# Two transformer blocks on one core: operand tiles at multiples of 512 bytes, and the second block's constants made in its own phase

## The chip, the cores and the metric

The kernel runs on one core of one Trainium2 chip. The metric is the device time of one execution in microseconds. Before the change the median of three runs is 2538.58 us (2537.44 to 2539.23).

## The reference

Two transformer blocks work one after the other on x, 256 tokens by 2,048 features, in fp32. Each block makes six modulation vectors from a condition c by a product of silu(c) with a 2,048 x 12,288 matrix ("ada"), normalizes and modulates x, mixes the tokens, adds the result through a gate, and then does the same with a feed-forward layer of width 8,192.

```python
# first block
mod = silu(c) @ w_ada + b_ada
h = rms_norm(x, norm1_w) * (1 + scale1) + shift1
u_pool, q, k, v, g_a, g_b = split(h @ w_in)
y_a = multiscale_pool(u_pool, w_pool, pool_scale) @ w_a_up
y_b = stick_breaking_attention(rms_norm(q), rms_norm(k), v) @ w_b_up
x = x + gate1 * ((sigmoid(g_a) * y_a + sigmoid(g_b) * y_b) @ w_o)
h2 = rms_norm(x, norm2_w) * (1 + scale2) + shift2
x = x + gate2 * (square(relu(h2 @ w_ff1)) @ w_ff2)
# second block: the same frame; the mixer is
attn = rms_norm(dilated_attention(rope(rms_norm(aq)), rope(rms_norm(ak)), av))
ho = hgrn2(gq, gf, gi, lb)          # gated recurrence; lb is the floor of its forget gate
mix = concat(attn, rms_norm(ho) * silu(gg)) @ w_out
```

## The kernel before, in words

*The products.* All large products stream the weights. A weight block of 128 partitions x 4 x 512 columns (1 MB) is loaded from HBM into a `raw` tile (4 buffers, `pump`, line 163, queue of SP). Half a block at a time is split into two parts whose sum it is: `hi`, the rounded part, by a copy on ScalarE (line 199), and `lo`, the rest, by a subtraction on VectorE (line 207); there are four buffers of each. The activations are split in the same way, transposed to [feature, token], and kept in tiles `act` (modulated norm, and the operand of the output projections), `f` (hidden activations of the feed-forward layers), `pT` (pooling), `oT` (stick-breaking attention) and `m0` (a part of the second block's mixer). `unit` (line 292) issues, for each of the two token tiles, three matmuls of 128 x 128 weights against 512 columns: line 301 takes the activation's high part as weights and `hi` as the moving operand, line 302 the high part and `lo`, line 303 the low part and `hi`. A half block is two contraction tiles, so 12 matmuls.

*The order.* `run` (line 243) emits the program by half blocks. Before each one it runs the functions that `at` registered for it, steps the generators in `side` (spawned work such as attention heads), and prepares `hi` and `lo` up to three half blocks ahead (`LOOK`). Around a norm four half blocks are taken together, one token tile after the other. The modulation vectors are products on VectorE (`ada_product`, line 175) that are spread over the weight blocks.

*The constants of the second block.* `block2_consts` (line 879) is a generator that is spawned at half block 40 of the first feed-forward layer (line 1419). It loads masks (`lvl`, `cnt`), positions, inverse frequencies and rotary weights by five DMAs on SP's queue, converts the masks on VectorE, builds the rotary tables (`rope`, two sines on ScalarE) and the floor of the forget gate (`lb`). Results lie in the pool `fix2`, opened at the start of the first feed-forward layer (line 408) and kept to the end; scratch is a tile `consts` of the pool `t2p`.

*The stick-breaking heads* (`sb_head`, line 846) work in a tile of three rows of 384 columns: e, lb and lm. The sums over later keys are a product of lm with the triangle `tri` and with the matrix `ones`, two of the three 128-column parts of `cst`, whose first is the identity `ident` of all transposes.

*Where tiles lie.* A pool's tiles lie one behind the other in the order of their first request, pools in the order in which they are opened; each tile's size is rounded up to 32 bytes. The fixed pool begins at byte 16,512 of each partition, with `cb` (8,192 bytes), `x` (16,384), `pkt` (1,184), `cst` (1,536). The starts of the operand tiles in the program of the kernel before:

| tile | role on lines 301 to 303 | first byte | modulo 512 |
|---|---|---|---|
| hi (4 buffers x 2 halves) | moving | 79,168 and on by 2,048 | 320 |
| lo (4 buffers x 2 halves) | moving | 95,552 and on by 2,048 | 320 |
| act (4 tiles) | weights | 128,320 and on by 8,192 | 320 |
| oT (2 tiles) | weights | 202,048 and 210,240 | 320 |
| pT (in the place of x) | weights | 24,704 | 128 |
| f (4 tiles) | weights | 172,000 and on by 8,192 | 480 |
| m0 (2 tiles) | weights | 172,000 and 180,192 | 480 |

Within a tile all slices that are taken as weights or as moving operand start at multiples of 512 bytes from its first byte. Memory ends at byte 229,376; the last tile of the first block's mixer ends at 229,184, the gate of the feed-forward layers at 229,344.

Of the kernel before, what the change touches and what calls it, by code (L numbers as in the profile page):

```python
# [18 lines left out]
P = 128  # L19
# [14 lines left out]
# packed parameter columns: name -> (first column, columns)  # L34
# [29 lines left out]
class Net:  # L64
    def __init__(self, ctx, tc, A):
# [10 lines left out]
        self.scope = ctx.enter_context(ExitStack())  # L76
        self.side = []
# [48 lines left out]
    def add_block(self, src, units):  # L126
        """units: four (segment, k) pairs, in the order of the block's 512-column tiles."""
# [13 lines left out]
    def add_pair(self, srcs, a, b):  # L141
        """Two segments side by side, two contraction tiles of each in turn."""
# [38 lines left out]
    def prep_hi(self):  # L181
        """The first part of the next half block; what stands before it in the queue is used first."""
# [20 lines left out]
    def prep_lo(self):  # L203
        """The rest of that half block."""
# [16 lines left out]
    def interleave(self, plan):  # L221
        """Spread the vector products over the weight blocks: (first block, blocks per product, items)."""
# [89 lines left out]
    def act_tiles(self):  # L312
        """Lazily allocated [feature, token] operand of 16 contraction tiles, split in two parts."""
# [12 lines left out]
    def rstd(self, ss, n, d, out=None):  # L326
        """(ss/d + eps)^-1/2 of a [128, n] tile of sums of squares, with a Newton step."""
# [13 lines left out]
    def split_to(self, src, dst):  # L341
        """Transpose four 128-column tiles of src [token, feature] into dst [feature, 4, 2, token]."""
# [7 lines left out]
    def gate_rows(self, col, dst):  # L350
        """dst[:, n] = gate n on every partition, from gate columns [128, 16]."""
# [9 lines left out]
    def mod_cols(self, mod, b, j0, name):  # L361
        """mod + b_ada columns j0..j0+15."""
# [4 lines left out]
    def load_c2(self):  # L367
        """c_2 on every partition, in the place of c."""
# [15 lines left out]
    def residual(self, g, a, tt, gate, norm=None):  # L384
        """x[:, group g] += gate * acc for one token tile; sums of squares for the norm that follows."""
# [13 lines left out]
    def ffn(self, w1p, w1, w2, norm, mod, b, ada_base, next_norm=None, out=None):  # L399
# [83 lines left out]
    def setup(self):  # L483
        nc, fix, A = self.nc, self.fix, self.A
        # silu(c) on every partition: the row times a column of ones
# [16 lines left out]
        self.cst = fix.tile([P, 3, P], F32, tag="cst", name="cst")  # L502
# [4 lines left out]
        self.ident, self.tri, self.ones = (self.cst[:, i, :] for i in range(3))  # L507
# [15 lines left out]
    def block1(self):  # L523
# [9 lines left out]
        # ---- normalized x, transposed; its modulation arrives tile by tile  # L533
# [34 lines left out]
        # ---- twelve column groups, a chunk of the contraction tiles at a time  # L568
# [5 lines left out]
        def part(key):  # L574
            """Where the sums of a group are kept between its contraction chunks: [token, 2, 512]."""
# [49 lines left out]
        # where the vector products of the later chunks stand: first block, blocks per product  # L625
# [72 lines left out]
        # ---- output projection  # L698
# [62 lines left out]
    def pool_loads(self, i):  # L761
        """Half of the pooling weights; the window matrices with the first."""
# [19 lines left out]
    def pool_group(self, g, u, pT):  # L782
        """Windowed means minus the token, then the group's map, times the scale, in two parts."""
# [47 lines left out]
    def heads(self, hs, every, make):  # L831
        """Run the heads' generators, a new one every so many steps, at most two at once."""
# [13 lines left out]
    def sb_head(self, h, qkT, v, o32):  # L846
# [8 lines left out]
        w = mp.tile([P, 3, 384], F32, tag="band" if h % 2 else "wp", name="sbw")  # L855
        yield
        e, lb, lm = (w[:, i, :] for i in range(3))
# [20 lines left out]

    def block2_consts(self):
        """Masks, rotary tables, the decay floor: everything of the second block that is small."""  # L880
        nc, fix, A = self.nc, self.fix2, self.A
        self.lvl = fix.tile([P, 7, 64], U8, tag="lvl", name="lvl")
# [10 lines left out]
        pos = fix.tile([P, 2], I32, tag="pos", name="pos")  # L893
        nc.sync.dma_start(out=pos, in_=A["positions"])
        tmp = self.t2(name="consts")
        w = tmp[:, 0:192].rearrange("p (a t f) -> p a t f", a=6, t=2)
        inv = tmp[:, 192:208]
        nw = tmp[:, 208:272].rearrange("p (a f) -> p a f", a=2)
# [650 lines left out]
```

## Time and profile before

| | us |
|---|---|
| median of three runs | 2538.58 |
| lowest and highest | 2537.44, 2539.23 |
| span of the profiled execution | 2536.3 |
| TensorE busy | 2505.9 |
| VectorE busy | 1808.3 |
| ScalarE busy | 1268.3 |

The span is the time from the first to the last instruction of one profiled execution, which is some 2 us less than the time of a run. The busy time of TensorE counts a matmul from its start to the modelled end of its last result, so that neighbours overlap: the recorded duration of a matmul (some 390 ns) is longer than the distance from its start to the start of the next (some 230 ns), and the throughput is read from the starts. Weight loads have rows of their own (PEld). In the rows below, a stretch shows its start and end, its us, the busy us and instructions of TensorE, its weight loads, VectorE, ScalarE and GpSimd, then the granted share of TensorE's clock, the DMA engines' busy share and GB/s; where it is of one tile alone, VectorE and ScalarE only.

### The profile page before, as it was taken

The page shows a single profiled execution, that of the slowest core. Times are in us where ns is not written, and L with a number is a line of the kernel's source. Part 1 is how long each engine was busy: PE and PEld are TensorE (multiplying, and loading weights), DVE is VectorE, ACT ScalarE, POOL GpSimd, SP SyncE. Part 2 cuts the span into 40 slices and gives each one's busy share as a digit, 9 for nine tenths or more (in the row PEclk, how much of TensorE's full clock was granted, in tenths as well). Part 3 has the DMA queues.
Part 4 walks back from the last instruction along what each step waited for, and adds up shares of the span by engine and source line. Part 5 has one row for each costly group of instructions (what it writes and reads, how often), then busy time and mean ns, then how long its engine had stood idle before and what let it go on. Part 6 is the DMA issues. An engine that isn't in the chain of part 4 may idle for free.

```text
span 2536.3 us, 29315 instructions
## 1 busy us (share of the span) xinstructions
PE 2505.9 (99%) x11392; PEld 2052.5 (81%) x11392; DVE 1808.3 (71%) x2121; ACT 1268.3 (50%) x1740; POOL 4.0 (0%) x8
## 2 busy tenths in 40 slices
PE   7999999999999999999999999999999999999999
PEld 5778888887888888888887888888788888888887
DVE  7897888888866677787777878766666554446554
ACT  5536545445545534534446656565554453443442
POOL 0000000000000000000000000000000000000000
PEclk9999999999999999999999999999999999999999
DMA  9988678977877777787766564665576755555553
GB/s 358 374 321 317 241 298 316 396 283 286 303 306 291 297 298 299 288 324 300 297 266 239 226 231 184 234 231 215 200 265 253 271 189 183 182 184 194 186 191 124
DMA packets 92876, 662.08 MB, mean 261 GB/s; under 512 B 10689, under 2 KB 11329, under 8 KB 12737
## 3 DMA queue, kind: packets, MB, share of 16 engines
q1 hardware_dynamic: 92738, 660.22, 68.8%
q8 instruction: 89, 1.46, 0.2%
q14 instruction: 49, 0.40, 0.0%
HBM read 655.99 MB, written 4.19 MB: 260 GB/s over the span
## 4 chain that ended last, share of the span: by engine, by line
PE 90%; DVE 6%; ACT 2%; issue 1%; DMA 1%; SPq 0%; ACTq 0%; DVEq 0%
PE acc L303 28%; PE acc L302 28%; PE acc L301 28%; DVE ada L175 2%; DVE lo L207 2%; PE ms L346 1%; ACT hi L199 1%; PE ms L1169 1%; PE ms L850 1%; PE ms L1283 0%; DMA raw<-in_win 0%; ACT hm L1387 0%; PE ms L1401 0%; PE ms L357 0%; PE ms L757 0%
## 5 line engine op out<-in xcount | busy, mean ns | idle before, releaser
L207 DVE TENSOR_TENSOR lo<-raw,hi 128x1024 fp32r<-128x1024 f32 x848 | 1027.9, 1223 | 615.6 <-ACT hi L199 612.7
L199 ACT CAST hi<-raw 128x1024 fp32r<-128x1024 f32 x848 | 883.0, 1049 | 879.8 <-PE acc L303 831.4
L301 PE MATMUL acc<-hi,act 128*128 128x512 f32 x2208 | 875.6, 397 | 8.0 <-ACT hi L199 6.9
L302 PE MATMUL acc<-lo,act 128*128 128x512 f32 x2208 | 863.8, 391 | 9.2 <-DVE lo L207 9.2
L303 PE MATMUL acc<-hi,act 128*128 128x512 f32 x2208 | 862.8, 391 | 0.0
L302 PEld LDWEIGHTS acc<-lo,act 128*128 128x128 f32 x2208 | 416.0, 188 | 98.5 <-DVE lo L207 16.5
L301 PEld LDWEIGHTS acc<-hi,act 128*128 128x128 f32 x2208 | 415.7, 188 | 93.7 <-ACT hi L199 8.8
L303 PEld LDWEIGHTS acc<-hi,act 128*128 128x128 f32 x2208 | 415.6, 188 | 88.2 <-DVE act L1392 0.7
L175 DVE CUSTOM_DVE_ANT_0 ada<-ada,cb 128x2048 f32<-128x2048 f32 x192 | 438.2, 2284 | 0.0
L303 PE MATMUL acc<-hi,f 128*128 128x512 f32 x1024 | 408.3, 399 | 0.0
L302 PE MATMUL acc<-lo,f 128*128 128x512 f32 x1024 | 403.6, 394 | 0.0
L301 PE MATMUL acc<-hi,f 128*128 128x512 f32 x1024 | 402.3, 393 | 0.0
L302 PEld LDWEIGHTS acc<-lo,f 128*128 128x128 f32 x1024 | 192.3, 188 | 49.4
L301 PEld LDWEIGHTS acc<-hi,f 128*128 128x128 f32 x1024 | 192.2, 188 | 45.6
L303 PEld LDWEIGHTS acc<-hi,f 128*128 128x128 f32 x1024 | 192.2, 188 | 44.3
L380 ACT ACTIVATE act<-xT,sAB 128x256 fp32r<-128x256 f32 x16 | 9.6, 601 | 86.9 <-DVE sAB L560 86.9
L418 ACT ACTIVATE relu<-acc 128x512 f32<-128x512 f32 x64 | 37.7, 590 | 29.0 <-PE acc L303 29.0
L348 DVE TENSOR_TENSOR f<-ms,f 128x512 fp32r<-128x512 f32 x64 | 41.1, 683 | 3.7 <-ACT f L347 3.7
L391 DVE TENSOR_TENSOR res<-acc,gate 128x512 f32<-128x512 f32 x32 | 22.0, 688 | 29.9 <-PE acc L303 29.9
L394 ACT ACTIVATE res<-x 128x512 f32<-128x512 f32 x24 | 15.2, 632 | 53.1 <-DVE x L392 53.1
L347 ACT CAST f<-ms 128x512 fp32r<-128x512 f32 x64 | 34.4, 589 | 14.5 <-PE ms L346 14.5
L419 ACT ACTIVATE relu<-relu 128x512 f32<-128x512 f32 x64 | 40.5, 633 | 2.0
(242 smaller groups left out, 1292.8 us busy)
## 6 DMA issues: line engine op xcount, KB each, us to landing
raw<-in_ff SPq DMA_DIRECT2D x240, 1024.0 KB, 5.8
ada<-in_ada SPq DMA_DIRECT2D x192, 1024.0 KB, 5.9
raw<-in_win SPq DMA_DIRECT2D x120, 1024.0 KB, 6.7
raw<-in_ff1p SPq DMA_DIRECT2D x16, 1024.0 KB, 5.5
raw<-in_wa SPq DMA_DIRECT2D x8, 1024.0 KB, 6.9
raw<-in_wb SPq DMA_DIRECT2D x8, 1024.0 KB, 9.5
raw<-in_wop SPq DMA_DIRECT2D x8, 1024.0 KB, 6.9
raw<-in_wo SPq DMA_DIRECT2D x8, 1024.0 KB, 8.6
```

The costliest lines, as they stand in the source:

```text
L175: self.nc.vector.tensor_tensor_reduce(out=t, in0=t, in1=cb(), scale=1.0, scalar=0.0, op0=ALU.mult, op1=ALU.add, accum_out=mod[:, j:j + 1])
L199: self.nc.scalar.copy(hi, src)
L207: self.nc.vector.tensor_tensor(out=lo, in0=src, in1=hi.bitcast(F32), op=ALU.subtract)
L301: self.nc.tensor.matmul(a, xh, hi, start=first, stop=False)
L302: self.nc.tensor.matmul(a, xh, lo, start=False, stop=False)
L303: self.nc.tensor.matmul(a, xl, hi, start=False, stop=last)
L346: nc.tensor.transpose(ps[:, i, :], src[:, i * P:(i + 1) * P], self.ident)
L347: nc.scalar.copy(dst[:, :, 0, :], ps)
L348: nc.vector.tensor_tensor(out=dst[:, :, 1, :], in0=ps, in1=dst[:, :, 0, :].bitcast(F32), op=ALU.subtract)
L418: nc.scalar.activation(r, acc[tt], AF.Relu)
L419: nc.scalar.activation(r, r, AF.Square)
L850: mm = lambda *a, **kw: nc.tensor.matmul(*a, skip_group_check=True, **kw)
```

## The change

Unnamed padding tiles of 96 and 72 columns are put into the fixed pool; `cst` loses its third part, in whose place `ones` becomes a column of ones that is read with step 0. The heads' tile has two rows instead of three: lm is written into e, and the sum goes into lb. The pool `fix2` is opened with the second block's phase (and lives as long as that), with a padding tile of 88 columns at its head; `block2_consts` is spawned at the second block's first half block, with its scratch in a tile under the tag of the later `A1` (1,536 columns). In it the five DMAs come first, then the floor `lb`, then the masks, then the rotary tables. The comments and docstrings that the diff also removes are left out here.

```diff
@@ Net.__init__
         self.scope = ctx.enter_context(ExitStack())
+        self.fix.tile([P, 96], F32, tag="pad0", name="pad")
@@ ffn
         def pools():
-            self.scope.close()
-            if ada_base == 0:
-                self.fix2 = self.ctx.enter_context(self.tc.tile_pool(name="fix2", bufs=1))
             self.phase(fp=4, ffp=1)
@@ setup
         self.pkt = fix.tile([P, NPK], F32, tag="pk", name="pkt")
-        self.cst = fix.tile([P, 3, P], F32, tag="cst", name="cst")
+        fix.tile([P, 72], F32, tag="pad1", name="pad")
+        self.cst = fix.tile([P, 2, P], F32, tag="cst", name="cst")
...
-        self.ident, self.tri, self.ones = (self.cst[:, i, :] for i in range(3))
+        self.ident, self.tri = (self.cst[:, i, :] for i in range(2))
+        one = fix.tile([P, 1], F32, tag="one", name="one")
+        nc.vector.memset(one, 1.0)
+        self.ones = one.to_broadcast([P, P])
@@ sb_head
-        w = mp.tile([P, 3, 384], F32, tag="band" if h % 2 else "wp", name="sbw")
+        w = mp.tile([P, 2, 384], F32, tag="band" if h % 2 else "wp", name="sbw")
...
-        nc.vector.tensor_tensor(out=lm, in0=lb, in1=z, op=ALU.subtract)
+        nc.vector.tensor_tensor(out=e, in0=lb, in1=z, op=ALU.subtract)
         yield from lag(4)
         sf = self.ms([P, 384])
-        mm(sf, self.tri, lm, start=True, stop=False)
-        mm(sf[:, P:S], self.ones, lm[:, S:], start=False, stop=True)
+        mm(sf, self.tri, e, start=True, stop=False)
+        mm(sf[:, P:S], self.ones, e[:, S:], start=False, stop=True)
         yield
+        e = lb
         nc.vector.tensor_tensor(out=e, in0=sf, in1=lb, op=ALU.add)
@@ block2_consts
-    def block2_consts(self):
+    def block2_consts(self, mt):
         nc, fix, A = self.nc, self.fix2, self.A
+        fix.tile([P, 88], F32, tag="pad", name="pad")
+        raw = mt([P, 1536], "A1", "consts")
+        masks = raw[:, 0:448].rearrange("p (a b) -> p a b", a=7), raw[:, 448:832]
...
+        for t, name in zip(masks, ("lvl", "cnt")):
+            nc.sync.dma_start(out=t, in_=A[name])
+        nc.sync.dma_start(out=pos, in_=A["positions"])
+        nc.sync.dma_start(out=inv, in_=A["inv"])
+        nc.sync.dma_start(out=nw, in_=A["rope_w"].partition_broadcast(P))
...
+        yield from lag(6)
...
+        yield from lag(2)
         self.lvl = fix.tile([P, 7, 64], U8, tag="lvl", name="lvl")
         self.cnt = fix.tile([P, 384], U8, tag="cnt", name="cnt")
-        for dst, name in ((self.lvl, "lvl"), (self.cnt, "cnt")):
-            t = self.t2(dst.shape, name="mask")
-            nc.sync.dma_start(out=t, in_=A[name])
-            yield from lag(6)
+        for dst, t in zip((self.lvl, self.cnt), masks):
             nc.vector.tensor_copy(dst, t)
...
@@ block2
-        self.at(first, lambda: self.phase(mixp=1))
+        self.at(first, lambda: self.phase(fix2=1, mixp=1))
+        self.at(first, lambda: self.spawn(self.block2_consts(mt)))
@@ net
-            n.at(first + 40, lambda: n.spawn(n.block2_consts()))
```

## Rows read from the trace of the kernel before

**Rows 1.** The page: busy time of engines, the chain by line, ScalarE's weight copies.

```profile
PE 2505.9 (99%) x11392; PEld 2052.5 (81%) x11392; DVE 1808.3 (71%) x2121; ACT 1268.3 (50%) x1740; POOL 4.0 (0%) x8
...
PE acc L303 28%; PE acc L302 28%; PE acc L301 28%; DVE ada L175 2%; DVE lo L207 2%; PE ms L346 1%; ACT hi L199 1%; PE ms L1169 1%; PE ms L850 1%; PE ms L1283 0%; DMA raw<-in_win 0%; ACT hm L1387 0%; PE ms L1401 0%; PE ms L357 0%; PE ms L757 0%
...
L199 ACT CAST hi<-raw 128x1024 fp32r<-128x1024 f32 x848 | 883.0, 1049 | 879.8 <-PE acc L303 831.4
```

**Rows 2.** TensorE's waits in the whole run: total us, times, longest.

```profile
PE acc L302 <- DVE lo L207: 9.2, 17, 0.8
PE acc L301 <- ACT hi L199: 6.9, 3, 2.8
```

**Rows 3.** TensorE's instructions in time (start us, duration us): act and oT.

```profile
54.70 0.39 PE L303 MATMUL acc<-hi,act 128*128 128x512 f32 x1
...
94.85 0.39 PE L303 MATMUL acc<-hi,act 128*128 128x512 f32 x1
...
425.39 0.39 PE L301 MATMUL acc<-hi,oT 128*128 128x512 f32 x1
...
436.05 0.39 PE L303 MATMUL acc<-hi,oT 128*128 128x512 f32 x1
```

**Rows 4.** The same view: first and last of runs with f, pT and m0.

```profile
1099.82 0.39 PE L301 MATMUL acc<-hi,f 128*128 128x512 f32 x1
...
1139.95 0.39 PE L302 MATMUL acc<-lo,f 128*128 128x512 f32 x1
...
319.05 0.40 PE L302 MATMUL acc<-lo,pT 128*128 128x512 f32 x1
...
325.59 0.40 PE L303 MATMUL acc<-hi,pT 128*128 128x512 f32 x1
...
1757.51 0.39 PE L301 MATMUL acc<-hi,m 128*128 128x512 f32 x1
...
1762.88 0.39 PE L303 MATMUL acc<-hi,m 128*128 128x512 f32 x1
```

**Rows 5.** Instructions by tile: duration ns min/median/max, first and last start us.

```profile
L303 PE MATMUL acc<-hi,act x2208: 387/389/628, 23.1 to 2440.7; 128*128 128x512 f32 x184
L303 PE MATMUL acc<-hi,oT x64: 389/389/395, 425.8 to 514.9; 128*128 128x512 f32 x64
L303 PE MATMUL acc<-hi,f x1024: 388/399/399, 703.5 to 2531.2; 128*128 128x512 f32 x171
L303 PE MATMUL acc<-hi,pT x64: 392/394/398, 319.3 to 372.8; 128*128 128x512 f32 x64
```

**Rows 6.** Instructions of line 348, VectorE's writes into f and act.

```profile
L348 DVE TENSOR_TENSOR f<-ms,f x64: 678/682/692, 659.7 to 2445.6; 128x512 fp32r<-128x512 f32 x64
L348 DVE TENSOR_TENSOR act<-ms,act x8: 679/684/693, 494.7 to 527.9; 128x512 fp32r<-128x512 f32 x8
```

**Rows 7.** Stretches, the tile consts alone, lvl, table loads, SP, waits, DMA sizes.

```profile
740.00:770.00 30.00, 30.00 (x130) 24.12 (x129) 23.69 (x56) 15.76 (x18) 0.00 (x0) 1.00 0.70 264
1345.00:1366.00 21.00, 20.72 (x99) 16.81 (x98) 15.42 (x24) 14.44 (x22) 0.00 (x0) 1.00 0.75 292
...
733.00:766.00 33.00, 4.34 (x33) 0.68 (x3) 1.00 0.71 266
...
734.29 0.39 DVE L888 CAST lvl<-mask 128x448 uint8<-128x448 f32 x1
...
L115 ACT ACT_TABLE_LOAD x2 | 2.6, 1283 | 0.0
...
745.98 0.42 SPq L894 DMA_DIRECT2D pos<-in_positions  x1
...
SPq L163 <- DVE lo L207: 62.7, 12, 8.8
...
PE acc L302 <- DVE lo L207: 0.9, 2, 0.7
...
mask<-in_lvl SPq DMA_DIRECT2D x1, 224.0 KB, 7.2
```

More of the change, by code (lines that the diff above doesn't have):

```diff
@@ L854, in sb_head @@
         mm(z[:, S:], self.mb16[:, 1, :], self.mb16[:, 0, :], start=False, stop=True)
-        w = mp.tile([P, 3, 384], F32, tag="band" if h % 2 else "wp", name="sbw")
+        w = mp.tile([P, 2, 384], F32, tag="band" if h % 2 else "wp", name="sbw")
         yield
-        e, lb, lm = (w[:, i, :] for i in range(3))
+        e, lb = (w[:, i, :] for i in range(2))
         nc.scalar.activation(e, z, AF.Abs)
@@ L877, in sb_head @@
         nc.scalar.copy(o32[:, h, :], o)
-    def block2_consts(self):
+    def block2_consts(self, mt):
         nc, fix, A = self.nc, self.fix2, self.A
+        fix.tile([P, 88], F32, tag="pad", name="pad")
+        raw = mt([P, 1536], "A1", "consts")
+        masks = raw[:, 0:448].rearrange("p (a b) -> p a b", a=7), raw[:, 448:832]
+        w = raw[:, 832:1024].rearrange("p (a t f) -> p a t f", a=6, t=2)
+        inv = raw[:, 1024:1040]
+        nw = raw[:, 1040:1104].rearrange("p (a f) -> p a f", a=2)
+        lw = raw[:, 1104:1128].rearrange("p (a f) -> p a f", a=3)
+        pos = fix.tile([P, 2], I32, tag="pos", name="pos")
+        for t, name in zip(masks, ("lvl", "cnt")):
[3 more added lines that the diff above has]
+        nc.sync.dma_start(out=nw, in_=A["rope_w"].partition_broadcast(P))
+        self.lb = fix.tile([P, 2, NH], F32, tag="lb", name="lb")
+        l0, l1 = self.pk("hg_lb_logits_2", 0, 8), self.pk("hg_lb_logits_2", 8, 8)
+        e0, e1, mx = (lw[:, i, :] for i in range(3))
+        yield from lag(6)
+        nc.vector.tensor_tensor(out=mx, in0=l0, in1=l1, op=ALU.max)
+        nc.vector.tensor_tensor(out=e0, in0=l0, in1=mx, op=ALU.subtract)
+        nc.vector.tensor_tensor(out=e1, in0=l1, in1=mx, op=ALU.subtract)
+        yield
+        self.tables("exp")
+        nc.scalar.activation(lw[:, 0:2, :], lw[:, 0:2, :], AF.Exp)
+        nc.vector.tensor_tensor(out=mx, in0=e0, in1=e1, op=ALU.add)
+        nc.vector.reciprocal(mx, mx)
+        nc.vector.tensor_tensor(out=self.lb[:, 0, :], in0=e0, in1=mx, op=ALU.mult)
+        nc.vector.tensor_scalar(out=self.lb[:, 1, :], in0=self.lb[:, 0, :], scalar1=-1.0, scalar2=1.0,
+                                op0=ALU.mult, op1=ALU.add)
+        yield from lag(2)
         self.lvl = fix.tile([P, 7, 64], U8, tag="lvl", name="lvl")
         self.cnt = fix.tile([P, 384], U8, tag="cnt", name="cnt")
-        for dst, name in ((self.lvl, "lvl"), (self.cnt, "cnt")):
-            t = self.t2(dst.shape, name="mask")
-            nc.sync.dma_start(out=t, in_=A[name])
-            yield from lag(6)
+        for dst, t in zip((self.lvl, self.cnt), masks):
             nc.vector.tensor_copy(dst, t)
@@ L892, in block2_consts @@
         nc.vector.tensor_scalar(out=self.off, in0=self.off, scalar1=-NEG, scalar2=None, op0=ALU.mult)
[L893 to L898, printed above, removed]
-        lw = tmp[:, 272:296].rearrange("p (a f) -> p a f", a=3)
-        nc.sync.dma_start(out=inv, in_=A["inv"])
-        nc.sync.dma_start(out=nw, in_=A["rope_w"].partition_broadcast(P))
-        yield from lag(6)
+        yield
         pf, ang, kk, r, sn, cs = (w[:, i, :, :] for i in range(6))
@@ L938, in block2_consts @@
             nc.vector.memset(self.wq[0:32, i:i + 1], f)
-        yield
-        self.lb = fix.tile([P, 2, NH], F32, tag="lb", name="lb")
-        l0, l1 = self.pk("hg_lb_logits_2", 0, 8), self.pk("hg_lb_logits_2", 8, 8)
-        e0, e1, mx = (lw[:, i, :] for i in range(3))
-        nc.vector.tensor_tensor(out=mx, in0=l0, in1=l1, op=ALU.max)
-        nc.vector.tensor_tensor(out=e0, in0=l0, in1=mx, op=ALU.subtract)
-        nc.vector.tensor_tensor(out=e1, in0=l1, in1=mx, op=ALU.subtract)
-        yield
-        self.tables("exp")
-        nc.scalar.activation(lw[:, 0:2, :], lw[:, 0:2, :], AF.Exp)
-        nc.vector.tensor_tensor(out=mx, in0=e0, in1=e1, op=ALU.add)
-        nc.vector.reciprocal(mx, mx)
-        nc.vector.tensor_tensor(out=self.lb[:, 0, :], in0=e0, in1=mx, op=ALU.mult)
-        nc.vector.tensor_scalar(out=self.lb[:, 1, :], in0=self.lb[:, 0, :], scalar1=-1.0, scalar2=1.0,
-                                op0=ALU.mult, op1=ALU.add)
     def block2(self, norm, next_norm):
@@ L1415, in net @@
             norm = n.block1()
-            first = len(n.subs)
             norm2 = Norm(n, "norm1_w_2", n.mod2, "b_ada_2", 0, 16, 96)
             n.ffn(A["ff1p_1"], A["ff1_1"], A["ff2_1"], norm, n.mod1, "b_ada", 0, next_norm=norm2)
-            n.at(first + 40, lambda: n.spawn(n.block2_consts()))
             norm3 = Norm(n, "norm2_w_2", n.mod2, "b_ada_2", 48, 64, 96)
@@ L1465, in pack @@
     r = np.arange(P)
-    cst = np.zeros((P, 3, P), np.float32)
+    cst = np.zeros((P, 2, P), np.float32)
     cst[:, 0] = np.eye(P)
     cst[:, 1] = r[:, None] > r[None, :]
-    cst[:, 2] = 1.0
     dev["mask"] = np.where(r[:, None] < r[None, :], 0.0, NEG).astype(np.float32)
```

## The prediction

> **What bounds the kernel now.** I read the page from the top: busy shares, the chain of work that ended last, then the costliest groups, and after them the waits of TensorE. TensorE is busy for 2505.9 of 2536.3 us, and the chain of waits runs for 84% over the three matmul lines 301 to 303 [rows 1]. ScalarE's copies of weights sit idle 879.8 us, 831.4 of them until TensorE gives a buffer back [rows 1]. So nearly everywhere the weights are ready before TensorE is; the exceptions are small: over the whole run TensorE waited 9.2 us for a lo part and 6.9 us for a hi part [rows 2]; the granted clock is 1.00, the upper level of 2.4 GHz, in the stretches shown [rows 7]. What counts is therefore how many nanoseconds lie between the starts of two matmuls of lines 301 to 303. There are 10,176 of them: 6,624 that take their stationary operand from act, 3,072 from f, 192 each from pT and oT, 96 from m0 (three lines of 2,208, 1,024, 64, 64 and 32 [rows 5]; the 32 from the loops).
>
> **The cadence depends on the tile.** All these matmuls have the same shape, 128 columns of weights against 512 of a hi or lo tile, and each has its own weight load. The rows that show starts give the spacing of undisturbed runs:
> - act: 54.70 to 94.85 us holds 178 matmuls, so 40.15 / 177 = 226.8 ns [rows 3].
> - oT: 425.39 to 436.05 us holds 48, so 10.66 / 47 = 226.8 ns [rows 3].
> - f: 1099.82 to 1139.95 us holds 173, so 40.13 / 172 = 233.3 ns [rows 4].
> - pT: 319.05 to 325.59 us holds 29, so 6.54 / 28 = 233.6 ns [rows 4].
> - m0: 1757.51 to 1762.88 us holds 24, so 5.37 / 23 = 233.5 ns [rows 4].
>
> The recorded durations say the same: on line 303 a median of 389 ns with act and oT, 399 with f, 394 with pT [rows 5].
>
> What separates the groups is the byte at which the stationary tile starts, taken modulo 512 (front part, table of placements): hi and lo are always at 320; act and oT are at 320 too; f and m0 at 480, pT at 128. Loop, shape, strides and writing engines are alike. It isn't the half of memory: oT at bytes 202,048 and up is quick, f between 172,000 and 204,768 is slow. It isn't an alignment of 64 bytes: pT at 128 has it and is slow. The simplest reading is that a matmul is quick when weights and moving tile have the same residue, and loses 6.67 ns otherwise.
>
> A rule of the skill speaks against this. The Trainium skill, TensorE: Matmul & The Clock Gate, section "Step-by-step: what each phase is for", says that TensorE has two independent read ports and that loading the next weights takes no read bandwidth from the running matmul. By that rule the place of act or f could not matter and this part of the sum would be zero. The rows don't agree: 226.8 against 233.3 ns with the same moving tiles.
>
> **The change part by part.**
> 1. *Placement.* 96 columns (384 bytes) before cb and 72 (288) after pkt, less 512 for the dropped third of cst, plus 32 for the new one, shift everything behind the fixed pool by 192: hi, lo, act, t2 go from 320 to 0. cb and x start 384 later, so pT goes from 128 to 0. f follows directly on t2, since the pool fix2 is no longer open in the first feed-forward block: 0. In the second block fix2 is filled to 3,072 bytes by the 88 columns, so m0, too, is at 0. (cst, at 448 by the same count, and mb16 aren't at multiples of 512; their products aren't on lines 301 to 303.) All residues are then equal, as act, oT and hi are now. Working: f, pT and m0 come to the cadence of act and oT: 3,072 x 6.67 = 20.5 us, 192 x 6.67 = 1.3 us, 96 x 6.67 = 0.6 us; sum 22.4 us. act and oT stay. All of it lies on the path, as TensorE has hardly any idle time in these stretches. Bounds, from the rivals below: 67.9 us more gain, or 45.5 us lost.
> 2. *Other engines at new addresses.* The write of the low part takes 682 ns into f and 684 ns into act [rows 6], though the residues differ: nothing for VectorE; likewise ScalarE. And TensorE waits for VectorE's lo only 9.2 us in all [rows 2].
> 3. *The constants move* from half block 40 of the first feed-forward block to the start of the second block. In 740 to 770 us, where most of their steps run now, TensorE is busy 30.00 of 30.00 us [rows 7]: taking them out gains nothing there. Put in, they are 4.34 us of VectorE and 0.68 us of ScalarE on the scratch tile, and four conversions for lvl, cnt and off of up to 0.39 us each [rows 7], about 5.8 us of VectorE in all; also one table load of 1.28 us (two of them go from the first feed-forward block) [rows 7]. By the order of the steps they fall between 1345 and 1366 us, where VectorE is busy 15.42 of 21 us [rows 7]: its 5.6 us of idle time there are just used up. Queued behind them on VectorE are the lo parts, which TensorE takes next, on ScalarE the hi parts; the sums for the forget floor wait on VectorE for the exponential on ScalarE, which can stand behind one hi copy. The cover is that lo is made three half blocks ahead, 36 matmuls or 8 us; without it the cost is the 5.8 us. I take one more wait like the longest that TensorE had for a lo part at this boundary, 0.7 us [rows 7], with 0 and 5.8 as bounds.
> 4. *Their five DMAs* now stand on SP's queue at that boundary. They need the space of the first two f tiles, last read four half blocks earlier, and put five issues of about 0.42 us and some 0.43 MB (224 KB for lvl, the rest mostly cnt), 1.5 us at 292 GB/s, ahead of the next weight loads [rows 7]. SP spends this time waiting for buffers anyway, 62.7 us on line 163 between 1315 and 1400 us [rows 7]; four raw buffers hide it. 0; uncovered 3.6 us.
> 5. *Small edits.* A memset of one column in the setup, a shorter cst load, lm written over e and the sum over lb in the stick-breaking heads: no new engine waits; the small products with ident, tri and ones keep their count. The broadcast column as weights is no new form: the gates' transposes use one. Taken as 0, a few tenths either way.
>
> Sum: 2536.3 - 22.4 + 0.7 = 2514.6 us for the span. The median of the runs, 2538.58, is 2.3 us above that span; with the same around it the forecast is 2516.9 us.
>
> **The rivals.**
> *The aligned place is quicker still.* f and pT lie at different distances from hi and lose the same 6.67 ns; if 0 is as far below 320 as equal residues are below unequal ones, all 10,176 matmuls lose another 6.67 ns: 67.9 us more, 2449 us. For it: a matmul may be slowed at 320 as well. Against: no run in the trace goes below 226.8, and between 320 and 0 lies a shift of all operands alike, which leaves their relation as it is. Chance 0.10. The Trainium skill, TensorE: Matmul & The Clock Gate, section "Wait — 56ns, not 53.3ns?", gives 215.7 ns for 512 columns back to back at full clock; by that figure, an estimate, 11 ns from each of 6,816 and 17.7 from each of 3,360 would go, 2404 us. No matmul of these lines shows it here.
>
> *320 is the good residue, not equality.* Of three stationary residues seen (128, 320, 480) only 320 is quick. If it is the residue itself that is quick, 0 may be like 128 and 480: act and oT slow down to 233.4, f stays. The price is 6,816 x 6.67 = 45.5 us: 2585 us, slower than before. It decides as soon as one act product at the new place runs at 233. For it: two of three are slow. Against: hi and lo would have no part in it, though they stream beside each load. Chance 0.08.
>
> *No gain.* f is slow for another reason, or the padding doesn't put the tiles where I count them (an unused tile might get no space), or the boundary to the second block eats half of it and more. Then 2533 to 2545 us, middle 2539. For it: I add up addresses that the trace doesn't show. Against: five tiles fit the reading, none contradicts it. Chance 0.10. (It is also the time that the rule on the two ports, above, would give.)
>
> **How the numbers follow.** Forecast 0.72, with 2508 to 2524 as its own range (22.4 us give or take a few tenths per matmul, and the 5.8 and 3.6 us uncovered). The rivals have 0.10, 0.08 and 0.10. The predicted time is the forecast's, 2516.9. To hold 0.8 the range takes in the forecast and most of the case without gain: high 2541; below, the part of the first rival that shows only a little of its gain: low 2498. A measurement of this kernel tells about 0.2% from no change, 5 us. Faster: forecast, first rival and a sliver of the third, 0.83. Same: 0.09. Slower: 0.08.
>
> **What would show it.** Right: durations of 389 ns on lines 301 to 303 with f, pT and m0; each of the eight stretches of 384 f products, now 384 x 233.3 = 89.6 us, shorter by 2.6 us; act unchanged at 226.8. If act falls below 226 the first rival holds; if act's median goes to 392 or more, the second; if f stays at 399 on line 303, the third. At the start of the second block TensorE's waits for lo and hi should stay near 1 to 2 us; more says that the moved constants cost. The prediction is wrong if equal residues are not what makes act quick.

## The result, and the profile after

| kernel | median, us | lowest, highest | ratio to before, 95% interval |
|---|---|---|---|
| before | 2538.01 | 2537.08, 2539.23 | |
| after | 2519.14 | 2517.71, 2521.38 | 0.9926 [0.9913, 0.9938] |

The change makes the kernel 0.74% faster. The profiled execution of after took 2517.71 us with a span of 2515.9 us, 20.4 us less than the span of before. The forecast was 2516.9 us, with 2514.6 us for the span. The profiled execution is the fastest of the four, so its span lies closer to the forecast (1.3 us above) than the median does (2.2 us above).

The page of after: busy time of the engines, the chain that ended last by line, and the costliest groups with ScalarE's copies of weights (line 199 before, 201 now) and VectorE's writes into f (348, now 350).

```profile
PE 2484.1 (99%) x11392; PEld 2053.3 (82%) x11392; DVE 1807.1 (72%) x2122; ACT 1266.9 (50%) x1739; POOL 4.0 (0%) x8
...
PE acc L303 28%; PE acc L305 28%; PE acc L304 28%; DVE lo L209 2%; DVE ada L177 2%; PE ms L348 1%; ACT hi L201 1%; PE ms L1176 1%; PE ms L853 1%; PE ms L1290 0%; ACT hm L1394 0%; DMA raw<-in_win 0%; PE ms L1408 0%; PE ms L359 0%; PE ms L760 0%
...
L201 ACT CAST hi<-raw 128x1024 fp32r<-128x1024 f32 x848 | 884.1, 1051 | 857.4 <-PE acc L305 820.8
...
L350 DVE TENSOR_TENSOR f<-ms,f 128x512 fp32r<-128x512 f32 x64 | 41.0, 683 | 3.7 <-ACT f L349 3.7
```

These answer to [rows 1] and [rows 6]. TensorE still sets the time (the lines 301 to 303 are now 303 to 305, again 84% of the chain); its busy time fell by 21.8 us with the same 11,392 instructions. VectorE and ScalarE take as long for the same instructions as before: 683 ns for a write into f against 682.

TensorE's instructions of after in time (start us, duration us), first and last of undisturbed runs with act, pT and f; they answer to [rows 3] and [rows 4].

```profile
54.50 0.39 PE L304 MATMUL acc<-lo,act 128*128 128x512 f32 x1
...
97.82 0.39 PE L303 MATMUL acc<-hi,act 128*128 128x512 f32 x1
...
317.59 0.40 PE L304 MATMUL acc<-lo,pT 128*128 128x512 f32 x1
...
323.95 0.39 PE L305 MATMUL acc<-hi,pT 128*128 128x512 f32 x1
...
704.37 0.40 PE L304 MATMUL acc<-lo,f 128*128 128x512 f32 x1
...
788.24 0.39 PE L305 MATMUL acc<-hi,f 128*128 128x512 f32 x1
```

The run with act holds 192 matmuls, so 43.32 / 191 = 226.8 ns, as before; pT 6.36 / 28 = 227.1 instead of 233.6; f 83.87 / 370 = 226.7 instead of 233.3. (The runs with m0 come to 226.6.) The recorded durations, by tile:

```profile
L305 PE MATMUL acc<-hi,f x1024: 388/390/395, 701.0 to 2510.8; 128*128 128x512 f32 x171
L305 PE MATMUL acc<-hi,act x2208: 386/390/632, 23.1 to 2422.9; 128*128 128x512 f32 x184
```

Against [rows 5], f came from a median of 399 ns to 390; act stands at 390 after 389, with the same distance from start to start.

From the starts of the first product of each tile, the whole execution divides into stretches. These are all that changed by more than 0.1 us (the first stretch of the second block is that from its first act product to the first m0 product):

| stretch | before, us | after, us | difference |
|---|---|---|---|
| start, up to the first pT product | 297.54 | 296.05 | -1.49 |
| pT | 54.29 | 53.27 | -1.02 |
| f, seven of the eight stretches | 90.48 (the last 90.25) | 87.93 (87.70) | -2.55 each |
| f, the last of the first block | 91.23 | 88.84 | -2.39 |
| second block, first stretch | 372.14 | 375.09 | +2.95 |
| m0, three stretches | 12.16, 5.60, 5.60 | 11.87, 5.44, 5.44 | -0.61 together |
| act between the m0 stretches | 36.39, 16.37 | 36.61, 16.43 | +0.28 together |

The eight f stretches give 7 x 2.55 + 2.39 = 20.24 us. So the operands gained 20.24 + 1.02 + 0.61 = 21.87 us; 2.95 us were lost in the second block, and 1.49 us were won at the start. Where the loss sits is seen in TensorE's waits of after between 1318 and 1700 us (total us, times, longest):

```profile
PE ms L1408 <- ACT xn L1381: 2.2, 3, 1.7
PE ms L1156 <- ACT qf L1041: 1.1, 1, 1.1
PE acc L304 <- DVE lo L209: 0.9, 2, 0.7
```

In before the same two lines (1401 and 1149) waited 0.3 us each. The wait for lo is what it was [rows 7].

### The profile page after: what moved, and what is told of

Same layout as the page of the kernel before. It is cut to its first block, busy times and chain, and to the rows that moved or that the text cites. A ratio compares the mean times of both kernels' runs of the same rounds, so it can differ in the third digit from the quotient of the medians.

```text
span 2515.9 us, 29325 instructions
## 1 busy us (share of the span) xinstructions
PE 2484.1 (99%) x11392; PEld 2053.3 (82%) x11392; DVE 1807.1 (72%) x2122; ACT 1266.9 (50%) x1739; POOL 4.0 (0%) x8
## 4 chain that ended last, share of the span: by engine, by line
PE 89%; DVE 7%; ACT 3%; issue 1%; DMA 1%; SPq 0%; ACTq 0%; DVEq 0%
PE acc L303 28%; PE acc L305 28%; PE acc L304 28%; DVE lo L209 2%; DVE ada L177 2%; PE ms L348 1%; ACT hi L201 1%; PE ms L1176 1%; PE ms L853 1%; PE ms L1290 0%; ACT hm L1394 0%; DMA raw<-in_win 0%; PE ms L1408 0%; PE ms L359 0%; PE ms L760 0%
## 5 line engine op out<-in xcount | busy, mean ns | idle before, releaser
L201 ACT CAST hi<-raw 128x1024 fp32r<-128x1024 f32 x848 | 884.1, 1051 | 857.4 <-PE acc L305 820.8
L303 PE MATMUL acc<-hi,f 128*128 128x512 f32 x1024 | 399.6, 390 | 0.0
L305 PE MATMUL acc<-hi,f 128*128 128x512 f32 x1024 | 398.8, 389 | 0.0
```

Source lines behind the costliest of these rows:

```text
L201: self.nc.scalar.copy(hi, src)
L303: self.nc.tensor.matmul(a, xh, hi, start=first, stop=False)
L305: self.nc.tensor.matmul(a, xl, hi, start=False, stop=last)
```

## The experiments

Three questions were open. Is it equality that makes an operand quick, or a good residue, and is 512 the period? Do the moved constants cost the 2.95 us? And what does the quick cadence depend on besides the place?

**e1_scan: the spacing by the places of both operands.** A microbenchmark with tiles of its own. For each case 12 groups of three matmuls run back to back, in the form of lines 303 to 305 (shortened; the line for `l` is like that for `h`):

```python
h = hi[:, m + 512 * (k // 2 % 2):m + 512 * (k // 2 % 2) + 512]   # m: moving residue / 4; lo likewise
a = o + 256 * (k % 8)                                            # o: residue of the weights / 4
xh, xl = w[:, a:a + 128], w[:, a + 128:a + 256]
nc.tensor.matmul(acc, xh, h, start=k == 0, stop=False)
nc.tensor.matmul(acc, xh, l, start=False, stop=False)
nc.tensor.matmul(acc, xl, h, start=False, stop=k == GROUPS - 1)
```

> This kernel leaves out all of the reference but x itself and runs only matmuls of the form of lines 301 to 303: 53 cases of 36, each case with one residue (start modulo 512 bytes) for the moving tiles and one for the weights: moving 0 with weights 0, 32 to 480; moving 320 with weights 0, 32 to 480; both equal at 32, 64 to 480; and six odd pairs at 8 and 16 bytes. Theory 1 (equality): 226.7 ns between starts in all cases of equal residues, about 233 to 234 in all others. Theory 2 (the multiple of 512 itself): 226.7 or less only where both stand at 0, and the equal cases at other places slower. Theory 3 (the place of the weights does not matter): one spacing in all cases. If the loss depends on the distance between the residues, the cases with moving 320 repeat those with moving 0, shifted by 320.

Its TensorE in time; the pairs of rows are 27 matmuls apart within one case. In this order: moving at 0 with weights at 32, 192 and 256, then both at 320.

```profile
21.03 0.40 PE L46 MATMUL acc<-hi,w 128*128 128x512 f32 x1
...
27.34 0.39 PE L46 MATMUL acc<-hi,w 128*128 128x512 f32 x1
...
62.98 0.39 PE L46 MATMUL acc<-hi,w 128*128 128x512 f32 x1
...
69.16 0.39 PE L46 MATMUL acc<-hi,w 128*128 128x512 f32 x1
...
79.60 0.39 PE L46 MATMUL acc<-hi,w 128*128 128x512 f32 x1
...
85.72 0.40 PE L46 MATMUL acc<-hi,w 128*128 128x512 f32 x1
...
229.82 0.39 PE L46 MATMUL acc<-hi,w 128*128 128x512 f32 x1
...
235.94 0.40 PE L46 MATMUL acc<-hi,w 128*128 128x512 f32 x1
```

6.31 / 27 = 233.7 ns, then 6.18 / 27 = 228.9, 6.12 / 27 = 226.7 and again 226.7. The table, and the other figures of the two microbenchmarks, are means over the last 27 intervals of a case, from starts in ns. Over all cases with multiples of 32 the spacing follows the distance (weights minus moving) modulo 256, whatever the moving residue:

| distance modulo 256 | 0 | 32 | 64 | 96 | 128 | 160 | 192 | 224 |
|---|---|---|---|---|---|---|---|---|
| ns from start to start | 226.7 | 233.4 | 233.4 | 234.3 | 232.4 | 233.3 | 228.9 | 233.3 |

All sixteen cases of equal residues from 0 to 480 settle at 226.7, 320 as well as 0, and none of the 53 cases lies below. So for starts at multiples of 32 equality decides, but with a period of 256 bytes where the prediction said 512, and the loss isn't one number: at 192 it is 2.2 ns. Before the change pT lay at 128 - 320, which is 64, and f and m0 at 160: both are places of the full loss, and so the tiles of before could not show the difference. A good residue of 320 and an aligned place quicker than 226.7 both fall.

**e2_f320: equal, but not at multiples of 512.** The change without its two pads in the fixed pool and with the old `cst`; hi, lo, act, oT, f and m0 all lie at 320, pT at 128.

```diff
-        self.fix.tile([P, 96], F32, tag="pad0", name="pad")
...
-        fix.tile([P, 72], F32, tag="pad1", name="pad")
-        self.cst = fix.tile([P, 2, P], F32, tag="cst", name="cst")
+        self.cst = fix.tile([P, 3, P], F32, tag="cst", name="cst")
...
```

> The changed kernel without its two padding tiles in the fixed pool and with the old cst: f, m0, act, oT, hi and lo all start at 320 modulo 512, pT at 128 as before; the constants stay where the change put them. Theory 1 (equality): f and m0 at 226.7 ns, only pT back at 233.5, so 1.3 us above the changed kernel's 2519.1: 2520.4. Theory 2 (the multiple of 512): f stays at 233.3, the gain is gone, and the moved constants still cost: 2538 to 2541.

2520.54 us (2519.72 to 2521.39), ratio 0.9934 [0.9919, 0.9950]. TensorE in time, pT and f:

```profile
318.58 0.40 PE L303 MATMUL acc<-lo,pT 128*128 128x512 f32 x1
...
325.11 0.40 PE L304 MATMUL acc<-hi,pT 128*128 128x512 f32 x1
...
706.35 0.40 PE L303 MATMUL acc<-lo,f 128*128 128x512 f32 x1
...
790.23 0.39 PE L304 MATMUL acc<-hi,f 128*128 128x512 f32 x1
```

f runs at 83.88 / 370 = 226.7 ns without any alignment to 512; pT, left at distance 64, at 6.53 / 28 = 233.2. What the change is named after is sufficient, not necessary: the distance between the operands counts.

**e3_act480: all products put at a bad distance.** The change with a pad of 80 columns ahead of hi and lo and one of 40 columns behind them: hi and lo at 320, act, f, oT and m0 at 480 (distance 160), pT at 0 (distance 192).

```diff
+        mk("pada", 1).tile([P, 80], F32, tag="pada", name="pad")
...
+        mk("padb", 1).tile([P, 40], F32, tag="padb", name="pad")
```

> The changed kernel with a padding of 320 bytes ahead of the hi and lo tiles and one of 160 behind them: hi and lo at 320, and act, f, oT and m0 all at 480, pT at 0, so all weights differ from the moving tiles, by the 160 bytes by which f differed before. Theory 1 (equality): all 10,176 matmuls at 233.3 instead of 226.7 ns, 67.9 us above the changed kernel: 2587. Theory 2 (what counts is each tile's own residue, 480 and 128 bad, 320 good): also slower by the same for the weights at 480. Theory 3 (the place does not matter, f was slow for another reason): 2519.

2574.17 us (2573.52 to 2574.81), ratio 1.0145 [1.0126, 1.0163]. TensorE in time, act and pT:

```profile
54.91 0.40 PE L306 MATMUL acc<-lo,act 128*128 128x512 f32 x1
...
110.69 0.39 PE L305 MATMUL acc<-hi,act 128*128 128x512 f32 x1
...
321.45 0.40 PE L306 MATMUL acc<-lo,pT 128*128 128x512 f32 x1
...
327.87 0.39 PE L307 MATMUL acc<-hi,pT 128*128 128x512 f32 x1
```

act runs at 55.78 / 239 = 233.4 ns, pT at 6.42 / 28 = 229.3, near the 228.9 that the microbenchmark has for this distance. The dependence on the distance is confirmed, also on act, whose distance the change itself leaves at 0. The time is 13 us below what was expected, in part since a slower matmul costs its full price only where TensorE waits for nothing: the pure act stretches of the feed-forward layers grew by 2.5 us each (89.72 to 92.24), as worked out, but the start, with 1,152 matmuls, grew by 3.9 us instead of 1,152 x 6.67 = 7.7, and the second block's first stretch by 5.4 us instead of 1,344 x 6.67 = 9.0. There the slower matmuls partly fill what had been waits: at the start TensorE waited 9.3 us for hi and lo instead of 11.4, in the second block's stretch 3.9 us in all instead of 5.4. That is some 2.1 and 1.5 us of the missing 3.8 and 3.6; where the rest went isn't shown, and the start alone varies by up to 3.6 us between executions (below).

**e4_late: the rotary tables 18 steps later.** After the masks, the generator of the constants rests for 19 steps instead of one before the angles, the sines and the 16 writes of `rope`.

```diff
         nc.vector.tensor_scalar(out=self.off, in0=self.off, scalar1=-NEG, scalar2=None, op0=ALU.mult)
-        yield
+        yield from lag(19)
```

> The changed kernel with the angles, the sines and the rotary tables of the constants put off by 18 steps (nine half blocks), behind the norm's last chunk; masks and floor stay. Theory A (the moved steps stand in VectorE's queue ahead of the norm's modulation and so hold up the activations): TensorE's 1.7 us wait for xn goes, 1.5 to 2.5 us less than the changed kernel, 2517. Theory B (the loss of some 3 us at the second block comes from the five DMAs or the clock, not from these steps): the same 2519.

2518.45 us (2517.00 to 2520.62), ratio 0.9926 [0.9913, 0.9938]. TensorE's waits between 1318 and 1700 us:

```profile
PE ms L1156 <- ACT qf L1041: 2.4, 1, 2.4
...
PE ms L1408 <- ACT xn L1381: 0.3, 1, 0.3
```

The wait for xn is gone, so the moved steps (angles, sines and writes together) had made it. But they now stand between 1371.9 and 1380.2 us, ahead of the next steps on VectorE, and the wait for qf grew from 1.1 to 2.4 us. The two waits are 2.7 us together instead of 3.3, and yet the stretch takes 375.63 us, no less than the 375.09 of after. TensorE's product behind the wait, and the stretch from 1388 to 1391 us, show why:

```profile
1386.35 0.38 PE L1156 MATMUL ms<-qf,key 128*128 128x128 f32 x1 [2.41 <-ACT qf L1041]
...
1388.00:1391.00 3.00, 3.00 (x11) 2.52 (x11) 3.00 (x4) 2.77 (x4) 0.00 (x0) 0.50 0.00 0
```

After this wait the granted clock was 0.50, the lower level of 1.2 GHz, and only 11 matmuls stand in these 3 us, where after has 22 at 1.00. Counted from the first product of the stretch, TensorE was 2.1 us behind the run e6_late62 (below) when the wait ended, and 3.7 us when the clock was back: 1.6 us went to the clock. So the work was moved from one busy place to another, and the longer single wait cost more than its own length. The expected 2517 us was not reached; against the 2519.14 of after the time shows no difference.

**e5_undo: the placement alone.** The constants go back to the first feed-forward layer, and only the layout stays. With `fix2` open there again and filled to 3,072 bytes, one pad of 8 columns in the fixed pool suffices: hi, lo, act, oT, f and m0 lie at 384, pT at 128, which is 256 away.

```diff
-        self.fix.tile([P, 96], F32, tag="pad0", name="pad")
...
-        fix.tile([P, 72], F32, tag="pad1", name="pad")
+        fix.tile([P, 8], F32, tag="pad1", name="pad")
...
+            self.scope.close()
+            if ada_base == 0:
+                self.fix2 = self.ctx.enter_context(self.tc.tile_pool(name="fix2", bufs=1))
...
-        self.at(first, lambda: self.phase(fix2=1, mixp=1))
-        self.at(first, lambda: self.spawn(self.block2_consts(mt)))
+        self.at(first, lambda: self.phase(mixp=1))
...
+            n.at(first + 40, lambda: n.spawn(n.block2_consts()))
```

> Placement kept, the move of the constants undone: they are made in the first feed-forward block again, the pool fix2 opens there with its 88 columns, the two pads of the fixed pool become one of 8 columns. By the addresses hi, lo, act, oT, f and m0 then lie at 384 modulo 512 and pT at 128, which is 256 away. Theory A (the move alone costs the 2.95 us that the second block's first stretch gained): that stretch, from its first act product to the first m0 product, falls from 375.1 to between 372.1 and 372.8 us, nothing is added in the first feed-forward block, and the time is 2519.1 - 2.6 = 2516.5 us. Theory B (the 2.95 us come from the new addresses): the stretch stays at 375 and the time at 2519. On pT: if the period is 256 bytes, as in the microbenchmark, pT runs at 226.7 ns; if it were 512 in the kernel, 233.4 ns and 1.0 us more.

2516.31 us (2515.93 to 2516.70), ratio 0.9911 [0.9896, 0.9926]. TensorE's waits between 1318 and 1700 us:

```profile
PE ms L1405 <- ACT xn L1378: 0.3, 1, 0.3
PE ms L1153 <- ACT qf L1038: 0.3, 1, 0.3
```

Both waits are gone. Its TensorE in time: first and last of a run with pT, and the first act and first m0 product of the second block.

```profile
319.73 0.40 PE L303 MATMUL acc<-lo,pT 128*128 128x512 f32 x1
...
326.08 0.39 PE L304 MATMUL acc<-hi,pT 128*128 128x512 f32 x1
...
1326.38 0.50 PE L302 MATMUL acc<-hi,act 128*128 128x512 f32 x1
...
1698.30 0.48 PE L302 MATMUL acc<-hi,m 128*128 128x512 f32 x1
```

The stretch of the second block takes 371.92 us, 3.17 us less than in after, and no stretch of the first feed-forward layer grew: f 87.93, act 89.72 us, as in after. So it was the move that cost the 3 us, and where the constants had been made, they cost nothing. This run also has other addresses than after; e6_late62 finds the same stretch at the addresses of after. pT at distance 256 runs at 6.35 / 28 = 226.8 ns: the period of 256 bytes holds in the kernel too.

**e6_late62: the constants where there is room.** As e4_late, with 62 steps.

```diff
-        yield
+        yield from lag(62)
```

> The changed kernel with 62 steps instead of one between the masks and the rotary tables, so that the angles, the two sines and the 16 writes of rope come at about 1455 us, after the first products of the recurrence's decay and before the first use of rope at 1490.7 us. Theory A (these steps stood ahead of the norm's chain on VectorE and then ahead of the chain to qf): both waits, for xn and for qf, return to about 0.3 us, the stretch falls from 375.1 to between 372.1 and 373.5 us, and the time is about 2516.9 us; one or two table loads more on ScalarE are hidden. Rival (VectorE has no slack anywhere in this stretch, the work only moves the wait, as with 19 steps): another wait of 1 to 3 us appears after 1455 us and the time stays at 2518 to 2520 us.

2515.94 us (2515.02 to 2518.24), ratio 0.9909 [0.9892, 0.9925]. TensorE's waits between 1318 and 1700 us, then the ends of the stretch:

```profile
PE ms L1408 <- ACT xn L1381: 0.3, 1, 0.3
PE ms L1156 <- ACT qf L1041: 0.3, 1, 0.3
```

```profile
1327.89 0.50 PE L303 MATMUL acc<-hi,act 128*128 128x512 f32 x1
...
1699.81 0.48 PE L303 MATMUL acc<-hi,m 128*128 128x512 f32 x1
```

371.92 us, the same as with the constants in the first block. The writes of `rope` now run from 1453.9 to 1455.2 us, after the first products of the decay, and one more table load on ScalarE (27 instead of 26) isn't seen in the time. The rival, that VectorE has no slack for them anywhere in this stretch, falls. Since the DMAs, the floor and the masks stay at the boundary in this kernel, they cost nothing there; the angles, the sines and the writes of `rope` cost all of it. By their medians e5_undo and e6_late62 are the fastest kernels here; their intervals overlap with that of after, and it is the stretch in the trace that shows the 3.2 us.

**e7_scan2: what else the quick cadence needs.** The microbenchmark again, with offsets below 32 bytes, weights whose two parts lie at different residues, fewer moving columns, and 64 weight columns.

```diff
-                    h = hi[:, m + 512 * (k // 2 % 2):m + 512 * (k // 2 % 2) + 512]
+                    h = hi[:, m + 512 * (k // 2 % 2):m + 512 * (k // 2 % 2) + n]
...
-                    xh, xl = w[:, a:a + 128], w[:, a + 128:a + 256]
+                    xh, xl = w[:, a + oh:a + oh + c], w[:, a + 128 + ol:a + 128 + ol + c]
```

> A microbenchmark; of the reference it computes nothing, the output is a copy of x. 38 cases of 12 groups of three matmuls, as lines 303 to 305, with a weight load each; moving tiles hi and lo at multiples of 512 bytes plus an offset, high and low weights at offsets of their own; then fewer moving columns (384, 256, 128) and 64 weight columns. Offsets 4, 8, 16, 24 and 176 to 248: distances near 0 and 192 show whether the good places are single points or flat. Mixed residues (high weights at 0, low weights at 32, 128 or 192): theory A, the loss arises while the next weights are loaded beside the running moving tile: the long interval lies between the second and the third matmul of a group, the others stay at 226.7 ns, mean 228.9 for distance 32; theory B, it arises in the matmul with its own weights: the long interval lies between the third and the next group's first. Columns: if the loss belongs to each load, it stays near 6.7 ns with 256 columns; if it belongs to each column streamed, it halves.

The run holds 37 cases, not 38. TensorE in time, 27 matmuls apart: both operands at 16; then 384 moving columns with the weights at distance 32.

```profile
172.32 0.40 PE L50 MATMUL acc<-hi,w 128*128 128x512 f32 x1
...
178.62 0.40 PE L50 MATMUL acc<-hi,w 128*128 128x512 f32 x1
...
228.30 0.34 PE L50 MATMUL acc<-hi,w 128*128 128x384 f32 x1
...
232.98 0.34 PE L50 MATMUL acc<-hi,w 128*128 128x384 f32 x1
```

Equal residues that aren't multiples of 32 aren't quick: 6.30 / 27 = 233.3 ns at 16, and 237.8 and 231.4 at 4 and 8. The same case at 16 had 231.1 in e1_scan: differences of 2 ns between such places aren't to be read finely, as each microbenchmark was run once. The quick distance 0 has no flanks: 4 to 24 bytes above it are 230 to 233.3 ns, 16 and 8 below it 228.3 and 233.3; beside 192, 188 and 196 are at 233.3.

With 384 columns all three distances tried (0, 32, 192) give 4.68 / 27 = 173.3 ns; with 256 columns it is 120.0 at distance 0 and 118.5 and 117.8 at 32 and 192, with 128 columns 111.7 to 111.8. So the loss belongs neither to each load nor to each column, as the two theories had it: of the four widths it was seen with 512 columns alone, and at 256 equality is even the slowest of the three. With 64 weight columns and 512 moving ones, equality gives 230.0 ns, distance 32 gives 231.4 and distance 192 gives 228.2.

The mixed residues decide nothing either. With only the low weights at 32, the mean is 233.3 ns, and the intervals after the first, second and third matmul of a group are 232.0, 239.0 and 229.0: the long interval is where theory A put it, but its mean was to be 228.9. With the low weights at 128 or 192 (means 231.1 and 230.9) the longest interval follows the third matmul, where theory B put it; with only the high weights at 32 the mean is 231.9. One displaced matmul of three slows its neighbours as well, so that neither the load beside the running matmul nor the matmul with its own weights can be named as the place.

## Why the prediction was right, and where it was off

*Placement* (step 1 of the sum) held in size: 20.24 us on f against 20.5, 1.02 on pT against 1.3, 0.61 on m0 against 0.6; together 21.87 against 22.4. The 0.3 us missing on pT are probably at its products around norms and heads, which the spacing alone doesn't bind; this wasn't followed up. The reading behind it, equal residues, is right; its two details, the modulus and the constant loss of 6.67 ns, are not: the period is 256 bytes, and the loss depends on the distance. Equal starts off the multiples of 32 bytes aren't quick either, which these tiles couldn't show. For this change all this was without effect, as all distances became 0 at multiples of 32. The choice of equality over a good residue rested on five tiles; after (equal at 0), e2_f320 (equal at 320) and e3_act480 (unequal) show it with the same products at other places.

*Other engines* (step 2) held: 683 against 682 ns, and 1051 against 1049 for ScalarE's copies.

*The moved constants* (step 3) are the term that was mis-sized: 0.7 us were put in, 2.95 measured against before and 3.17 against e5_undo, within the bounds of 0 to 5.8. What failed is the sentence that the cover is the lo parts made three half blocks ahead. That cover held: TensorE waited as long for lo as before. But lo isn't all that is queued behind the constants on VectorE. ScalarE and VectorE of after between 1350 and 1359 us, beside the TensorE product that waits:

```profile
1350.67 1.28 ACT L117 ACT_TABLE_LOAD   x1
...
1354.21 1.23 DVE L209 TENSOR_TENSOR lo<-raw,hi 128x1024 fp32r<-128x1024 f32 x1 [1.24 <-ACT hi L201]
1355.35 0.17 DVE L954 TENSOR_TENSOR rope<-consts 128x16 f32<-128x16 f32 x1
...
1356.63 0.17 DVE L958 TENSOR_TENSOR rope<-consts 128x16 f32<-128x16 f32 x1
1356.74 0.53 DVE L383 TENSOR_SCALAR hm<-ms,sA,shiftc 128x256 f32<-128x256 f32 x1
...
1357.30 0.56 ACT L382 ACTIVATE act<-ms,shiftc,sA 128x256 fp32r<-128x256 f32 x1 [2.66 <-DVE hm L383]
1357.77 1.32 ACT L1381 ACTIVATE xn<-x,nr 128x512 f32<-128x512 f32 x2
...
1358.53 0.33 PE L1408 MATMUL ms<-cst,xn 128*128 128x128 f32 x1 [1.68 <-ACT xn L1381]
```

The sixteen small writes stand ahead of the modulation's `hm` on VectorE. ScalarE sat 2.66 us until `hm` came, with the `xn` of the next 512 features queued behind it in its own order; TensorE's transpose of `xn` came after a wait of 1.68 us, and with it all products behind it in TensorE's order. The same two steps in e6_late62, where the constants are out of the way:

```profile
1356.78 1.32 ACT L1381 ACTIVATE xn<-x,nr 128x512 f32<-128x512 f32 x2
...
1360.38 0.60 PE L1408 MATMUL ms<-cst,xn 128*128 128x128 f32 x4
```

The first of these two `xn`, some 0.7 us long, is ready 2.9 us before TensorE takes it. So this chain of two engines has a lead of 2.9 us, against the 8 us that the prediction counted for lo. Counted from the first act product of the stretch (1324.19 us in after, 1327.89 in e6_late62), `xn` starts 33.6 us later in after and 28.9 in e6_late62: the constants held the chain up by 4.7 us, more than its lead. The sixteen writes, from 1355.35 to 1356.80 us, are 1.4 us of that. The other 3.3 had gathered before them: the arithmetic of the angles on VectorE, and on ScalarE the table load and the two sines, which stand ahead of the `hi` copy for which VectorE's `lo` waited 1.24 us. The runs move all these steps together, so what each of them costs alone isn't shown. e4_late shows the link by removing it. It shows too that the next chain, to qf, is tighter still: TensorE waits 0.3 us for qf even in e5_undo and e6_late62. e6_late62 finds the place where there is room.

*The five DMAs* (step 4) were rightly put at 0. In after they are issued between 1331.99 and 1334.18 us; e6_late62, which has them at the same place, and e5_undo, which doesn't, need the same 371.92 us for the stretch.

*Small edits* (step 5) held at 0: the stretches with the stick-breaking heads are the same within 0.1 us (10.88 and 21.76 us).

The sum gave 2514.6 us for the span, and 2515.9 was measured. Of the 2.3 us missing on the constants (2.95 instead of 0.7) and the 0.5 on placement, 1.5 were made up by the start, which the prediction had no reason to touch and which isn't the change's doing; to that extent the closeness of the sum is luck. In the profiled executions of before, after, e2_f320, e4_late, e5_undo and e6_late62, whose starts do the same work, TensorE's waits for hi and lo before 320 us are 12.8, 11.4, 12.6, 12.4, 13.8 and 14.9 us, and the start takes 297.5, 296.1, 297.0, 296.1, 298.2 and 299.6 us: less these waits, 283.7 to 284.7 us each time. So the start varies mostly by how early weights are there. Why they came earlier or later in one execution than in another wasn't tried.

Of the rivals, the quicker aligned place (2449 us) and the good residue 320 (2585 us) fall with e1_scan and with act's unchanged 226.8 ns in after; no gain falls with f. The prediction drew the same time from the rule on two read ports in the Trainium skill, TensorE: Matmul & The Clock Gate, section "Step-by-step: what each phase is for". The traces contradict that conclusion: with 512 columns the place of the weights does count, 226.7 against 233.4 ns. Whether it is at the ports that the loss arises, e7_scan2 leaves open. The rival at 2539 us had its chance from the uncertainty of the addresses too, and the f run alone settles both. The part of that rival which said that the boundary eats some of the gain came true, to about a seventh of it.

## What to carry to other kernels

When many matmuls of one shape run back to back, compare their start-to-start spacing by operand tile; a few nanoseconds between tiles of the same shape can be the place of the tiles, and here, with 128 columns of weights against 512, weights and moving operand should start at the same multiple of 32 modulo 256 bytes. Measure it for the shape at hand: at 128, 256 and 384 columns it gave nothing.

A side job that goes into an in-order queue is priced by the tightest chain behind it, not by the chain that one knows to have a lead; put it where no norm or first product is on its way, and look again after moving it, since the wait may have moved too, and look at the granted clock behind the wait.

## What the runs showed of the hardware

The spacing of matmuls depends on the distance of the starts of weights and moving operand modulo 256 bytes, from 226.7 ns at 0 over 228.9 at 192 to 234.3 at 96, with weights of 128 columns loaded for each 512 columns streamed and a granted clock of 1.00. The traces before the change had shown two levels only.

The quick case was seen only with starts at multiples of 32 bytes: equal starts at 4, 8 and 16 gave 231 to 238 ns.

The effect doesn't scale down with the stream: 173.3 ns at 384 columns for three distances alike. Taking the slope from 384 to 512 columns at distance 0, (226.7 - 173.3) / 128 = 0.417 ns a column, each matmul carries 226.7 - 512 x 0.417 = 13 ns on top of its columns at distance 0. The Trainium skill, TensorE: Matmul & The Clock Gate, section "Wait — 56ns, not 53.3ns?", has some 2.5 ns there for back-to-back matmuls. In none of the cases run here, each with its own weight load, was it seen: the least is at 256 columns and distance 192, 117.8 - 256 x 0.417 = 11 ns.

A wait of TensorE can cost more than its length: after the 2.41 us in e4_late the granted clock stood at 0.50 between 1388 and 1391 us, with 11 matmuls where after has 22, and 1.6 us were lost on top. After the 1.68 us wait in after the clock stayed at 1.00.
